# A two-layer hybrid block on one core: Strassen-like combinations of the hidden values in parts among the matmul steps, their low halves in the block after next

## The chip, the cores and the metric

One Trainium2 chip, one of its cores. The metric is the device time of one execution in microseconds (us). Three runs of the kernel before took 2234.09, 2236.21 and 2236.96 us; their median, 2236.21 us, is the time to compare with.

## The reference

256 tokens of width 2048 pass through two layers. Each layer has a mixer (gated delta rule and a linear recurrence in the first, two attentions in the second) and then a feed-forward part of inner width 5632. The change lies in the feed-forward part alone:

```python
def swiglu(hn, w_gate, w_up, w_down):
    return (jax.nn.silu(hn @ w_gate) * (hn @ w_up)) @ w_down
...
        h = h + swiglu(rmsnorm(h, ffn_norm[layer]), ffn_w_gate[layer], ffn_w_up[layer], ffn_w_down[layer])
```

## The kernel before, in words

All data are float32. Every product of float32 tiles is made of three matmuls on a high part (rounded by a ScalarE cast) and a low part (what the rounding left, a VectorE subtraction): high by high, high by low, low by high. `Bank.add` (L417 to L419) issues these three matmuls twice per weight tile and output bank.

The feed-forward part of a layer (`ffn`) is a stream of **blocks**. A block of gate and up weights makes 512 inner values for all tokens (`values`: silu(gate) times up). A block of down weights adds inner values times weights to 1024 of the 2048 output columns (`residual`). Per layer the stream has four gate and up blocks and two down blocks, again four and two, then three and one (16 blocks, numbered 0 to 15 here), and one more down block outside the stream.

Most blocks do part of their product with seven multiplications in place of eight (`seven`; called sevens below). That needs, besides sums of weight tiles (L483 and L490, VectorE, the tile "T"), four **combinations** of the left-hand values: `combine` makes them with four VectorE instructions of 128x256 (L396), a ScalarE cast for their high half (L397) and a VectorE subtraction for their low half (L399). For gate and up blocks the left-hand values are X and the combinations are made once a layer. For down blocks they are the inner values, and the combinations are made of the inner values of two, two and one of the blocks of a group: five a layer, ten in all.

`turned` does this for the values of a block j, in the next block. `first` transposes the values on TensorE (L654) and copies them out with ScalarE (L657 the high half of hid; L662 plain copies into the tile "e", only where combinations are wanted). `second` subtracts on VectorE for hid's low half (L666) and runs `combine` up to its `yield`, which stands behind the cast. `third` runs the rest, L399. These three are put ahead of steps 2, 3 and 4 of the block.

A block with two sevens has 22 **steps**, numbered 0 to 21 here: three plain ones, four steps of the sevens, a plain one, five of the sevens, a plain one, five of the sevens, three plain ones. A plain step is 12 matmuls, a step of a seven 6. `spread` puts functions ahead of the step of a given number, and `stream` issues all of it in the order that is written: inside `manual_schedule` VectorE, ScalarE and TensorE each take their instructions in this order. `stream` looks ahead: before step n is multiplied, the load, the sum T and the high cast (L530) of the steps up to n + 3 are issued, and the low subtraction (L543) of those up to n + 2. So a function put at n stands on VectorE behind the low part of step n + 1, and on ScalarE behind the cast of step n + 2.

Blocks 1, 2, 7, 8 and 13 of each layer hold combinations. Blocks 3, 9 and 14 of each layer have the same steps as gate and up blocks, but none.

The tile of the combinations and the sums T share a tag with two buffers (`mx.tile(..., tag="T", bufs=2)`). The values live in a tile "e" with one buffer, which the next block's values take at its step 20.

Of the kernel before, what the change touches and what calls it, by code (L numbers as in the profile page):

```python
# [47 lines left out]
def body(tc, A, out):  # L48
# [89 lines left out]
    def run(gen):  # L138

        while True:  # L140
            try:
                next(gen)
            except StopIteration as e:
                return e.value
# [244 lines left out]
    def combine(f, r=None):  # L389

        c = mx.tile([128, 4, 2, 128], F32, name="cc4", tag="T", bufs=2)
        if r is None:
            r = fp.tile([128, 2, 4, 2, 128], F32R, name="comb", tag="comb", bufs=4)
        a11, a21, a12, a22 = (f[t][:, 2 * j:2 * j + 2] for j in range(2) for t in range(2))
        for i, x, y, op in ((0, a21, a22, ALU.subtract), (1, a11, a21, ALU.subtract), (2, c[:, 0], a11, ALU.subtract), (3, a12, c[:, 2], ALU.add)):
            V.tensor_tensor(out=c[:, i], in0=x, in1=y, op=op)  # L396
        S.copy(r[:, 0], c)  # L397
        yield
        V.tensor_tensor(out=r[:, 1], in0=c, in1=r[:, 0].bitcast(F32), op=ALU.subtract)  # L399
        return r  # L400
# [237 lines left out]
    def ffn(L, then, fin=None):  # L638

        gu, dn = A[f"gu{L}"], A[f"dn{L}"]  # L640
        cx, ch, acts, guard = {}, {}, [], [None]
        todo = {}

        def turned(hid, j, want):

            o = {}

            def first():
                a = todo.pop(j)
                o["P"] = []  # L650
                for t in range(2):
                    P = ms([128, 4, 128], "Ph")
                    for i in range(4):
                        PE.transpose(P[:, i], a[:, 2 * t, i * 128:(i + 1) * 128], tb["ident"])  # L654
                    o["P"].append((P, hid[:, 4 * j:4 * j + 4, :, t * 128:(t + 1) * 128]))
                for P, d in o["P"]:
                    S.copy(d[:, :, 0], P)  # L657
                if want:

                    o["f"] = [a[:, 2 * t + 1].rearrange("p (k n) -> p k n", n=128) for t in range(2)]  # L660
                    for t in range(2):
                        S.copy(o["f"][t], o["P"][t][0])  # L662

            def second():
                for P, d in o["P"]:
                    V.tensor_tensor(out=d[:, :, 1], in0=P, in1=d[:, :, 0].bitcast(F32), op=ALU.subtract)  # L666
                if want:
                    o["c"] = combine(o["f"])
                    next(o["c"])

            def third():
                if want:
                    ch[j] = run(o["c"])

            return [first, second, third]

        def spread(order, put):

# [44 lines left out]

            return bank_sums, half(0), half(1)

        b, late, turn = 0, None, None
        for groups, down in (((0, 2, 2, 2), (2, 2)), ((2, 2, 2, 2), (2, 2)), ((2, 2, 2), (1, 1))):
            piece = len(groups)
            hid = ogp.tile([128, 16, 2, T], F32R, name="hid", tag="hid")
            for j in range(piece + 2):  # L730
                put = {}
                add = lambda n, *f: put.setdefault(n, []).extend(f)

                if late:
                    add(1, late)
                if turn:
                    for n, f in zip((2, 3, 4), turn):
                        add(n, f)
                late = turn = None
                if j < piece:  # L740
                    ns = groups[j]
                    order, F, M = steps(lambda i, u, b=b: gu[b, u, i], lambda k: X[:, k],
                                        {m: lambda m=m: cx[m] for m in range(ns)}, 4, 3, 3)
                    if b == 0:
                        add(5, lambda: cx.update({0: combine_x(X[:, 0:4])}))
                        add(8, rstd)
                        add(10, lambda: cx.update({1: combine_x(X[:, 4:8])}))
                    if b == 1:
                        guard[0] = order[0]
                    bs, h0, h1, late = values(hid, j, F, M, ns)  # L750
                    turn = turned(hid, j, j < max(down))
                    b += 1
                else:
                    p = j - piece
                    if b == NB and p == 1:
                        break
                    order, F, M = steps(lambda i, u, u0=2 * (b - piece), p=p: dn[2 * p + i, u0 + u], lambda k, hid=hid: hid[:, k],
                                        {m: lambda m=m: ch[m] for m in range(down[p])}, piece, 3, 3)
                    bs, h0, h1 = residual(p, F, M)
                n = len(order)  # L760
                add(n - 2, bs)
                add(n - 1, h0)
                spread(order, put)
                acts.append(h1)
# [3 lines left out]
        if fin:  # L768
            hooks, last = {5: lambda: then(0), 6: lambda: then(1)}, (3, 1, 3)
        else:  # L770
            hooks, last = {}, ()
# [763 lines left out]
```

## Time and profile before

| | |
|---|---|
| median of three runs | 2236.21 us |
| the profiled execution's own time | 2232.66 us |
| its span, first to last instruction | 2230.8 us |
| TensorE matmul busy | 2205.7 us (99%) |
| VectorE busy | 1965.3 us (88%) |
| ScalarE busy | 1333.4 us (60%) |
| mean granted TensorE clock | 0.999 of 2.4 GHz |

PE is TensorE, DVE VectorE, ACT ScalarE. A row of the timeline reads: start in us from the span's start, how long, engine, line, operation, output and inputs, shapes, how many instructions are merged; in brackets the idle time of the engine before it and what ended that. A matmul's end is modelled and overlaps the next one's start, so the pace of TensorE is read from start to start.

### The profile page before, as it was taken

What the parts mean: (1) busy time and instruction counts of PE and PEld (TensorE: products, weight loads), DVE (VectorE), ACT (ScalarE), POOL (GpSimd) and SP (SyncE); (2) the same over time, 40 slices, a digit from 0 to 9 for tenths busy, and PEclk for the clock granted to TensorE, in tenths of its full rate; (3) what the DMA queues carried; (4) which work ended last, traced back from release to release, by engine and by line L of the source; (5) the groups of instructions that cost most, each with busy time, mean ns of one, the idle gap of its engine ahead of it and who ended that gap; (6) DMA issues with size and microseconds to landing.
All of it is one profiled execution on the core that took longest, in us unless ns stands there. A gap on an engine that the chain in (4) does not pass through costs nothing.

```text
span 2230.8 us, 30548 instructions
## 1 busy us (share of the span) xinstructions
PE 2205.7 (99%) x10960; PEld 1838.8 (82%) x10960; DVE 1965.3 (88%) x2664; ACT 1333.4 (60%) x1784; POOL 54.0 (2%) x66
## 2 busy tenths in 40 slices
PE   9999999999999999999999999999999999999998
PEld 8888888877888778888888888888778887888786
DVE  8899676779999999999996688857899999999998
ACT  6776664556655666466664554445666566655665
POOL 0000000000000000000000000000000000000000
PEclk9999999999999999999999999999999999999999
DMA  8545456667778777778665565566678777877784
GB/s 284 156 144 168 141 147 187 208 190 229 226 229 247 205 219 235 224 219 238 198 199 155 157 185 174 161 181 226 189 212 232 229 215 225 237 222 232 223 238 151
DMA packets 126569, 453.78 MB, mean 203 GB/s; under 512 B 14129, under 2 KB 15665, under 8 KB 126289
## 3 DMA queue, kind: packets, MB, share of 16 engines
q1 hardware_dynamic: 117488, 420.10, 59.1%
q0 software_dynamic: 8640, 31.46, 8.7%
q8 instruction: 86, 1.41, 0.3%
q14 instruction: 67, 0.54, 0.1%
q10 hardware_dynamic: 288, 0.27, 0.0%
HBM read 449.68 MB, written 2.10 MB: 203 GB/s over the span
## 4 chain that ended last, share of the span: by engine, by line
PE 93%; DVE 4%; issue 1%; ACT 1%; DMA 0%; DVEq 0%; ACTq 0%
PE F L418 16%; PE F L419 16%; PE F L417 16%; PE Pw L201 11%; PE Pw L206 5%; PE M L418 5%; PE M L419 5%; PE M L417 4%; PE Px L305 3%; PE Px L307 3%; PE Px L306 3%; PE Ph L654 1%; DVE cc L396 1%; DVE tlo L543 1%; DVE T L490 1%
## 5 line engine op out<-in xcount | busy, mean ns | idle before, releaser
L181 ACT CAST whi<-raw 128x1024 fp32r<-128x1024 f32 x267 | 279.6, 1051 | 280.7 <-PE Pw L201 83.2
L182 DVE TENSOR_TENSOR wlo<-raw,whi 128x1024 fp32r<-128x1024 f32 x267 | 325.6, 1221 | 115.1 <-PE Px L306 37.9
L201 PE MATMUL Pw<-X,whi 128*128 128x512 f32 x1088 | 388.5, 400 | 0.0
L530 ACT CAST whi<-raw 128x1024 fp32r<-128x1024 f32 x342 | 350.7, 1047 | 33.5 <-PE F L419 16.9
L206 PE MATMUL Pw<-X,wlo 128*128 128x256 f32 x1088 | 304.7, 280 | 0.1
L417 PE MATMUL F<-whi,X 128*128 128x512 f32 x698 | 273.0, 391 | 0.0
L419 PE MATMUL F<-whi,X 128*128 128x512 f32 x698 | 272.2, 390 | 0.0
L543 DVE TENSOR_TENSOR wlo<-raw,whi 128x1024 fp32r<-128x1024 f32 x202 | 246.0, 1220 | 13.0 <-PE F L418 6.4
L418 PE MATMUL F<-wlo,X 128*128 128x512 f32 x650 | 254.1, 391 | 0.1
L530 ACT CAST whi<-T 128x1024 fp32r<-128x1024 f32 x110 | 116.0, 1055 | 213.4 <-DVE T L490 97.3
L201 PEld LDWEIGHTS Pw<-X,whi 128*128 128x128 f32 x1088 | 204.2, 188 | 47.4 <-issue 0.5
L206 PEld LDWEIGHTS Pw<-X,wlo 128*128 128x128 f32 x1088 | 205.3, 189 | 1.5 <-DVE wlo L182 0.8
L530 ACT CAST thi<-raw 128x1024 fp32r<-128x1024 f32 x162 | 169.4, 1047 | 12.0 <-PE F L419 8.8
L543 DVE TENSOR_TENSOR tlo<-raw,whi 128x1024 fp32r<-128x1024 f32 x140 | 170.8, 1220 | 5.6 <-PE F L418 3.0
L417 PEld LDWEIGHTS F<-whi,X 128*128 128x128 f32 x698 | 131.1, 188 | 27.0 <-issue 0.2
L419 PEld LDWEIGHTS F<-whi,X 128*128 128x128 f32 x698 | 131.1, 188 | 26.8
L530 ACT CAST thi<-T 128x1024 fp32r<-128x1024 f32 x64 | 67.5, 1054 | 132.4 <-DVE T L490 62.6
L418 PE MATMUL F<-tlo,X 128*128 128x512 f32 x370 | 144.5, 391 | 0.2 <-DVE tlo L379 0.2
L418 PEld LDWEIGHTS F<-wlo,X 128*128 128x128 f32 x650 | 122.1, 188 | 26.5 <-DVE wlo L543 1.8
L490 DVE TENSOR_TENSOR T<-T,raw 128x1024 f32<-128x1024 f32 x116 | 141.6, 1221 | 1.2
L417 PE MATMUL F<-whi,hid 128*128 128x512 f32 x352 | 137.8, 392 | 0.0
L419 PE MATMUL F<-whi,hid 128*128 128x512 f32 x352 | 137.1, 389 | 0.0
(448 smaller groups left out, 4688.6 us busy)
## 6 DMA issues: line engine op xcount, KB each, us to landing
raw<-in_gu SPq DMA_DIRECT2D x352, 512.0 KB, 4.5
raw<-in_dn SPq DMA_DIRECT2D x176, 512.0 KB, 4.8
raw<-in_w0w SPq DMA_DIRECT2D x72, 512.0 KB, 3.7
raw<-in_wo SPq DMA_DIRECT2D x64, 512.0 KB, 4.0
raw<-in_w1w SPq DMA_DIRECT2D x64, 512.0 KB, 3.7
raw<-in_gu POOLq DMA_DIRECT2D x40, 512.0 KB, 8.4
raw<-in_w1x SPq DMA_DIRECT2D x32, 512.0 KB, 4.2
raw<-in_dn POOLq DMA_DIRECT2D x20, 512.0 KB, 8.9
```

The lines of the kernel that those rows point to most:

```text
L181: S.copy(hi, raw)
L182: V.tensor_sub(lo, raw, hi.bitcast(F32))
L201: PE.matmul(P.rearrange("p a b -> p (a b)"), hi[:, kk], X[:, k].rearrange("p a b -> p (a b)"), start=k == 0, stop=False)
L206: PE.matmul(P[:, 0], lo[:, kk], X[:, k, 0], start=False, stop=k == NK - 1)
L305: PE.matmul(Ps[t], x[:, 0, ts], hi[:, kk], start=k == 0, stop=False)
L306: PE.matmul(Ps[t], x[:, 0, ts], lo[:, kk], start=False, stop=False)
L417: PE.matmul(self.t, xh, hi[:, kk], start=self.i == kk == 0, stop=False)
L418: PE.matmul(self.t, xh, lo[:, kk], start=False, stop=False)
L419: PE.matmul(self.t, xl, hi[:, kk], start=False, stop=kk == 1 and self.i == self.n - 1)
L490: V.tensor_tensor(out=b["t"], in0=b["t"], in1=b[name], op=ALU.add)
L530: S.copy(y.hi, y.raw)
L543: V.tensor_sub(y.lo, y.raw, y.hi.bitcast(F32))
```

## The change

`combine` yields also behind its second and its third VectorE instruction. `turned` now returns two things: functions with their step numbers for the next block (first at 2, second at 3, and, where combinations are wanted, a part at 8 and a part at 14), and a function for step 2 of the block after that one. So `second` makes two of the four combinations, the third follows ahead of step 8, the fourth and the cast ahead of step 14, and the low half one block later, behind that block's own `first`.

```diff
--- before.py
+++ after.py
@@ -394,6 +394,8 @@
         a11, a21, a12, a22 = (f[t][:, 2 * j:2 * j + 2] for j in range(2) for t in range(2))
         for i, x, y, op in ((0, a21, a22, ALU.subtract), (1, a11, a21, ALU.subtract), (2, c[:, 0], a11, ALU.subtract), (3, a12, c[:, 2], ALU.add)):
             V.tensor_tensor(out=c[:, i], in0=x, in1=y, op=op)
+            if 0 < i < 3:
+                yield
         S.copy(r[:, 0], c)
         yield
         V.tensor_tensor(out=r[:, 1], in0=c, in1=r[:, 0].bitcast(F32), op=ALU.subtract)
@@ -668,11 +670,14 @@
                     o["c"] = combine(o["f"])
                     next(o["c"])
 
-            def third():
-                if want:
-                    ch[j] = run(o["c"])
-
-            return [first, second, third]
+            def part():
+                next(o["c"])
+
+            def last():
+                ch[j] = run(o["c"])
+
+
+            return {2: first, 3: second, **({8: part, 14: part} if want else {})}, [last] if want else []
 
         def spread(order, put):
 
@@ -723,7 +728,7 @@
 
             return bank_sums, half(0), half(1)
 
-        b, late, turn = 0, None, None
+        b, late, turn, rest, next_rest = 0, None, None, [], []
         for groups, down in (((0, 2, 2, 2), (2, 2)), ((2, 2, 2, 2), (2, 2)), ((2, 2, 2), (1, 1))):
             piece = len(groups)
             hid = ogp.tile([128, 16, 2, T], F32R, name="hid", tag="hid")
@@ -733,10 +738,11 @@
 
                 if late:
                     add(1, late)
-                if turn:
-                    for n, f in zip((2, 3, 4), turn):
-                        add(n, f)
-                late = turn = None
+                for n, f in (turn or {}).items():
+                    add(n, f)
+                add(2, *rest)
+                late, turn, rest = None, None, next_rest
+                next_rest = []
                 if j < piece:
                     ns = groups[j]
                     order, F, M = steps(lambda i, u, b=b: gu[b, u, i], lambda k: X[:, k],
@@ -748,7 +754,7 @@
                     if b == 1:
                         guard[0] = order[0]
                     bs, h0, h1, late = values(hid, j, F, M, ns)
-                    turn = turned(hid, j, j < max(down))
+                    turn, next_rest = turned(hid, j, j < max(down))
                     b += 1
                 else:
                     p = j - piece
```

The arithmetic and the instructions are the same; TensorE's, SyncE's and GpSimd's orders are unchanged. What moves on VectorE is shown for blocks 2 and 3 of the first layer. In the changed file the numbers of the lines that follow are higher: L543 becomes L545, L490 L492, L483 L485, L399 L401, L666 L668, L702 L707.

The first place is VectorE around steps 3 to 6 of block 2, first before:

```order
L543 TENSOR_TENSOR tlo<-raw_5329,whi 128x1024
L543 TENSOR_TENSOR wlo<-T,whi 128x1024
L666 TENSOR_TENSOR hid<-Ph,hid 128x4x128 x2
L396 TENSOR_TENSOR cc_5407<-e 128x256 x2
L396 TENSOR_TENSOR cc_5407<-cc_5407,e 128x256
L396 TENSOR_TENSOR cc_5407<-e,cc_5407 128x256
L490 TENSOR_TENSOR T<-T,raw_5387 128x1024
L543 TENSOR_TENSOR tlo<-raw_5387,thi 128x1024
L399 TENSOR_TENSOR comb<-cc_5407,comb 128x1024
L543 TENSOR_TENSOR wlo<-T,whi 128x1024
```
and now:

```order
L545 TENSOR_TENSOR tlo<-raw_5328,whi 128x1024
L401 TENSOR_TENSOR comb<-cc_5051,comb 128x1024
L545 TENSOR_TENSOR wlo<-T,whi 128x1024
L668 TENSOR_TENSOR hid<-Ph,hid 128x4x128 x2
L396 TENSOR_TENSOR cc_5407<-e 128x256 x2
L492 TENSOR_TENSOR T<-T,raw_5387 128x1024
L545 TENSOR_TENSOR tlo<-raw_5387,thi 128x1024
L545 TENSOR_TENSOR wlo<-T,whi 128x1024
```
The last two of the four combinations and their low half have left this place; the low half of the previous block's combinations (cc_5051) has come in ahead of step 4's low part.

The second place is VectorE around steps 9 to 16 of block 2, first before:

```order
L543 TENSOR_TENSOR wlo<-T,whi 128x1024
L543 TENSOR_TENSOR tlo<-raw,whi 128x1024
L483 TENSOR_TENSOR T<-raw_5480,raw 128x1024
L543 TENSOR_TENSOR wlo<-raw_5480,thi 128x1024
L543 TENSOR_TENSOR wlo<-T,whi 128x1024
L543 TENSOR_TENSOR tlo<-raw_5507,whi 128x1024
L490 TENSOR_TENSOR T<-T,raw 128x1024
L543 TENSOR_TENSOR wlo<-raw,thi 128x1024
L543 TENSOR_TENSOR tlo<-T,whi 128x1024
L490 TENSOR_TENSOR T<-T,raw_5543 128x1024
L543 TENSOR_TENSOR wlo<-raw_5543,whi 128x1024
```
and now:

```order
L545 TENSOR_TENSOR wlo<-T,whi 128x1024
L396 TENSOR_TENSOR cc_5407<-cc_5407,e 128x256
L545 TENSOR_TENSOR tlo<-raw,whi 128x1024
L485 TENSOR_TENSOR T<-raw_5477,raw 128x1024
L545 TENSOR_TENSOR wlo<-raw_5477,thi 128x1024
L545 TENSOR_TENSOR wlo<-T,whi 128x1024
L545 TENSOR_TENSOR tlo<-raw_5504,whi 128x1024
L492 TENSOR_TENSOR T<-T,raw 128x1024
L545 TENSOR_TENSOR wlo<-raw,thi 128x1024
L545 TENSOR_TENSOR tlo<-T,whi 128x1024
L396 TENSOR_TENSOR cc_5407<-e,cc_5407 128x256
L492 TENSOR_TENSOR T<-T,raw_5540 128x1024
```
The third combination stands behind step 9's low part, the fourth behind step 15's and ahead of the sum and of the low part of step 16 (`wlo<-raw_5540`, the row after the last one shown).

The third place is the start of block 3, which has no combinations, first before:

```order
L543 TENSOR_TENSOR tlo<-raw_5685,whi 128x1024
L543 TENSOR_TENSOR wlo<-T,thi 128x1024
L666 TENSOR_TENSOR hid<-Ph,hid 128x4x128 x2
L490 TENSOR_TENSOR T<-T,raw 128x1024
L543 TENSOR_TENSOR wlo<-raw,whi 128x1024
```
and now:

```order
L545 TENSOR_TENSOR tlo<-raw_5684,whi 128x1024
L401 TENSOR_TENSOR comb<-cc_5407,comb 128x1024
L545 TENSOR_TENSOR wlo<-T,thi 128x1024
L668 TENSOR_TENSOR hid<-Ph,hid 128x4x128 x2
L492 TENSOR_TENSOR T<-T,raw 128x1024
L545 TENSOR_TENSOR wlo<-raw,whi 128x1024
```
Here the low half of block 2's combinations (cc_5407) is one more instruction ahead of step 4's low part and of hid's low halves.

## Rows read from the trace of the kernel before

**Rows 1.** The page, part 1: TensorE's busy time, share and instructions.

```profile
PE 2205.7 (99%) x10960; PEld 1838.8 (82%) x10960; DVE 1965.3 (88%) x2664; ACT 1333.4 (60%) x1784; POOL 54.0 (2%) x66
```

**Rows 2.** Waits of TensorE: who waited for whom, us in total, times, longest.

```profile
PE M L418 <- DVE wlo L543: 3.7, 6, 0.6
PE F L418 <- DVE tlo L543: 3.6, 6, 0.6
...
PE M L418 <- DVE tlo L543: 2.4, 4, 0.6
PE F L418 <- DVE wlo L543: 2.4, 4, 0.6
```

**Rows 3.** Timeline of TensorE, block 2 of the first layer, steps 5 and 6.

```profile
531.01 0.39 PE L419 MATMUL M<-whi,comb 128*128 128x512 f32 x1
531.24 0.39 PE L417 MATMUL F<-thi,comb 128*128 128x512 f32 x1
532.22 0.50 PE L418 MATMUL F<-tlo,comb 128*128 128x512 f32 x1 [0.59 <-DVE tlo L543]
532.55 0.40 PE L419 MATMUL F<-thi,comb 128*128 128x512 f32 x1
...
533.48 0.39 PE L417 MATMUL M<-whi,comb 128*128 128x512 f32 x1
534.49 0.50 PE L418 MATMUL M<-wlo,comb 128*128 128x512 f32 x1 [0.62 <-DVE wlo L543]
```

**Rows 4.** Timeline of TensorE, the same block, step 16.

```profile
550.98 0.48 PE L418 MATMUL F<-wlo,X 128*128 128x512 f32 x1
551.30 0.40 PE L419 MATMUL F<-whi,X 128*128 128x512 f32 x1
```

**Rows 5.** Timeline of VectorE, the same block, steps 3 to 6, then 9 to 12.

```profile
523.68 1.22 DVE L543 TENSOR_TENSOR tlo<-raw,whi 128x1024 fp32r<-128x1024 f32 x1
524.97 1.23 DVE L543 TENSOR_TENSOR wlo<-T,whi 128x1024 fp32r<-128x1024 f32 x1
527.14 1.29 DVE L666 TENSOR_TENSOR hid<-Ph,hid 128x512 fp32r<-128x512 f32 x2 [0.95 <-ACT e L662]
...
529.01 0.42 DVE L396 TENSOR_TENSOR cc<-cc,e 128x256 f32<-128x256 f32 x1
529.47 0.42 DVE L396 TENSOR_TENSOR cc<-e,cc 128x256 f32<-128x256 f32 x1
529.81 1.22 DVE L490 TENSOR_TENSOR T<-T,raw 128x1024 f32<-128x1024 f32 x1
530.95 1.22 DVE L543 TENSOR_TENSOR tlo<-raw,thi 128x1024 fp32r<-128x1024 f32 x1
532.08 1.22 DVE L399 TENSOR_TENSOR comb<-cc,comb 128x1024 fp32r<-128x1024 f32 x1
533.22 1.22 DVE L543 TENSOR_TENSOR wlo<-T,whi 128x1024 fp32r<-128x1024 f32 x1
...
537.90 1.23 DVE L543 TENSOR_TENSOR wlo<-T,whi 128x1024 fp32r<-128x1024 f32 x1
...
540.17 1.22 DVE L483 TENSOR_TENSOR T<-raw,raw 128x1024 f32<-128x1024 f32 x1
```

**Rows 6.** Timeline of ScalarE, the same block: the combinations' cast and the next.

```profile
529.93 1.05 ACT L397 CAST comb<-cc 128x1024 fp32r<-128x1024 f32 x1 [1.39 <-DVE cc L396]
531.06 1.05 ACT L530 CAST whi<-T 128x1024 fp32r<-128x1024 f32 x1
```

**Rows 7.** Timeline of VectorE, block 3: the low parts of steps 5 and 16.

```profile
572.18 1.22 DVE L543 TENSOR_TENSOR wlo<-raw,whi 128x1024 fp32r<-128x1024 f32 x1
...
589.93 1.22 DVE L543 TENSOR_TENSOR tlo<-raw,thi 128x1024 fp32r<-128x1024 f32 x1
```

**Rows 8.** Timeline of TensorE, block 3: the matmuls that take these two low parts.

```profile
575.12 0.39 PE L418 MATMUL F<-wlo,comb 128*128 128x512 f32 x1
...
592.80 0.39 PE L418 MATMUL F<-tlo,X 128*128 128x512 f32 x1
```

## The prediction

> **What bounds the kernel now.** I read the page's busy times first: TensorE is busy for 2205.7 us of the 2230.8 us span, 99% [rows 1]. So at most 25.1 us lie in gaps that the page can see, and a change that leaves TensorE's instructions alone can only give back stalls. The second view is what TensorE waits for. In the feed-forward parts that is almost only VectorE's low parts of weight tiles (L543), 6 + 6 + 4 + 4 = 20 times, 3.7 + 3.6 + 2.4 + 2.4 = 12.1 us [rows 2]. Twenty is two for each of the ten blocks that make combinations, so the third view is the timeline of one of them, block 2 of the first layer. TensorE's pace there is 0.23 us from matmul to matmul (531.01 to 531.24). At step 5 it takes 0.98 us to the next start, 0.75 too many, and the one after that comes 0.33 later, 0.10 too many; at step 6 the gap is 1.01 us, 0.78 too many, and I count the same 0.10 behind it [rows 3]. At step 16 another gap is 0.32 us, 0.09 too many [rows 4]. Together 0.75 + 0.10 + 0.78 + 0.10 + 0.09 = **1.82 us per block, 18.2 us in ten**. That is more than the view of waits gives, since the modelled end of a matmul hides part of a stall; from here on I count starts.
>
> Why these steps: the low part of step 5 ends at 530.95 + 1.22 = 532.17 and TensorE starts at 532.22, 0.05 later [rows 3, 5]. Ahead of it VectorE has done hid's low halves, four combinations and a sum without a pause. The low part of step 6 stands behind the combinations' low half, L399. In block 3, which has the same steps but no combinations, the low part of step 5 ends at 573.40 and is taken at 575.12, 1.72 us later; at step 16 these are 591.15 and 592.80, 1.65 us [rows 7, 8]. So over these eleven steps VectorE's work and TensorE's are almost equal: the distance shrinks by 0.07 us. A block that is late at step 5 stays late; VectorE has no room in the middle of a block, and this decides what the change is worth.
>
> **The change, part by part.** The sum is made against the profiled execution, 2232.66 us; the median of the three runs is 3.55 us above it, and I take the saving from the median.
>
> *Out of steps 3 to 6.* Two of four combinations leave the place ahead of the sum. From the start of the third to that of the sum pass 529.81 - 529.01 = 0.80 us [rows 5]. The start of this stretch does not move, since L666 waits for ScalarE's copies there, which follow TensorE's transposes. So the low part of step 5 ends at 532.17 - 0.80 = 531.37, where TensorE without a stall wants it at 531.24 + 0.23 = 531.47: 0.10 us of room, 0.05 of which the handing over needs. The first stall goes, narrowly. L399 costs 533.22 - 532.08 = 1.14 us [rows 5], so step 6 is earlier by 0.80 + 1.14 = 1.94 us, against the 1.63 us (0.75 + 0.10 + 0.78) by which TensorE was held up there: the second stall goes too. ScalarE does not keep it: before, the cast of the sum began at 531.06, just after the sum's end at 531.03 and behind the combinations' cast [rows 5, 6]; now that cast is gone from there and the sum ends earlier.
>
> *Into steps 9 to 16.* Two combinations of 128x256 come in, one ahead of step 10's low part, one ahead of step 16's. Start to start such a one costs 529.81 - 529.47 = 0.34 us where the next does not wait for its result, and 529.47 - 529.01 = 0.46 where it does [rows 5]. What follows now is a weight tile's low part or sum, which does not, so I take 0.34, and keep 0.46 as the upper end; below, 0 would be one that hides in a pause, and rows 5 show VectorE without pauses between these steps, so I price that as a rival. By block 3's shape the room at step 16 is 0.10 - 0.07 - 2 x 0.34 = -0.65 us. With 0.05 to hand over and 0.10 for the restart, TensorE is held up by **0.80 us per block** in place of 1.82, at step 16, or in part some steps earlier, which does not change the total. That saves **1.02 us per block, 10.2 us in ten**.
>
> *The cast* of the combinations (L397, 1.05 us) now stands on ScalarE between the casts of steps 16 and 17. The cast of step 17 needs a sum that VectorE makes behind the fourth combination; that sum ends 0.34 + 1.22 - 0.42 = 1.14 us after the combination, and the cast of 1.05 us, begun 0.04 after it (529.93 against 529.47 + 0.42), is over by then, as it was in its old place [rows 5, 6]. I cost it at nothing; uncovered it would be 1.05 us.
>
> *The low half, one block on.* L399 stands ahead of step 4's low part and hid's low halves of the next block. In blocks 2 and 8 VectorE is idle for 0.95 us right behind step 4's low part, until ScalarE has copied [rows 5]. Step 3's low part starts at 523.68; with 1.14 for L399 step 4's starts at about 525.95 and is over at 527.18, and L666 starts at 527.14 now: covered to within a few hundredths. In blocks 3, 9 and 14 nothing covers it and everything behind is later by up to 1.14 us, but there TensorE's room is 1.65 us and more [rows 7, 8]. So nothing, in ten places. If the four blocks 2 and 8 of both layers had to pay it in full, it would be 4 x (1.14 + 0.10) = 5.0 us: the upper end.
>
> *What else is touched.* The combinations' tile now keeps one of the two T buffers into the next block, so the sevens' sums share the other. In block 2 the second seven's first sum starts at 540.17, and the last reader of the previous T is over at 537.90 + 1.23 = 539.13 [rows 5]: no wait. The values in "e" are read until ahead of step 14, and the tile is taken again at step 20. The queues of SyncE and GpSimd keep their order; a weight tile's buffer comes free up to 0.34 us later behind the pieces.
>
> **The sum.** 2232.66 - 10.2 = 2222.5 us for an execution like the profiled one, 2236.21 - 10.2 = **2226.0 us** for the median.
>
> **The rivals.** *A, every stall goes:* the pieces fall into pauses. Then 18.2 us come back, 2218.0 us. For it: the large stalls are at steps 5 and 6 alone. Against it: the 0.09 us at step 16 [rows 4] and the distance that shrinks from 1.72 to 1.65 in block 3 show that the middle has no pauses.
>
> *B, a piece costs its whole duration.* Two runs of VectorE's instructions overlap at their seams now: the combinations last 0.42 us and start 0.34 apart, L399 lasts 1.22 and the next starts after 1.14 [rows 5]. Should a piece between unlike instructions lose that overlap, each costs 0.42 or more, the stall grows by 2 x 0.08 = 0.16 us per block, and 1.6 us of the saving are lost: 2227.6 us; at 0.46 it is 0.24, and 2228.4. The Trainium skill has such a rule: in VectorE: DVE Perf Modes, section The DRAIN you can't avoid, the next instruction does not start until the pipe has emptied, so that only the number of instructions counts. The starts in this trace do not agree with it as it stands, being closer than the durations.
>
> *C, the low half is not covered one block on.* Its place is ahead of step 4's low part, its price 1.14 + 0.10 us, and it decides where the next block has less room than that. Paid in all ten next blocks it is 12.4 us, more than the 10.2 saved: 2236.2 + 2.2 = 2238.4 us, slower. For it: it stands ahead of hid's low halves, and steps 5 and 6 come right behind. Against it: 0.95 us of idle time in blocks 2 and 8, 1.65 us of room in the others [rows 5, 7, 8]. The four full prices alone give 2231.0 us.
>
> *D, nothing is won:* the stalls move whole to later steps. It would need the low half, too, to stay in its block; it leaves it, as the order shows. What stays of this case is that something unseen, such as a later landing of a weight tile, eats the saving: about 2236 us.
>
> **How the numbers follow.** Forecast 0.74, A 0.06, B 0.10, C 0.04, D 0.06. The range runs from 2222.0 (4 us under the forecast, as the three runs lie within 2.9 us of each other and the profiled one 3.55 under their median) to 2231.0, which takes in B and the four uncovered blocks; it leaves out A, C and D, 0.16. A measurement of this kernel can tell about 0.2%, 4.5 us, from no change. Faster by more than that, below 2231.7 us: the forecast, A and B, 0.90. Within it: most of D and half of C, 0.07. Slower: the rest, 0.03.
>
> **What would show it.** Right: in the ten blocks TensorE's gaps at steps 5 and 6 are gone or under 0.2 us, and gaps of 0.6 to 0.8 us in all stand at steps 11 to 16; VectorE's busy time unchanged; blocks 3, 9 and 14 as long as before. A shows as no gap at step 16. B shows as VectorE starting 0.42 or more after each lone combination. C shows as new gaps at steps 5 or 6 of blocks 2, 3, 8, 9 and 14. The forecast is wrong if the low part of step 5 is still waited for by more than 0.3 us, or if the gap at step 16 passes 1.5 us.

## The result and the profile after

Six runs of the changed kernel took 2220.22 to 2223.29 us, median **2220.81 us**; six of the kernel before on the same chip 2232.10 to 2236.96, median 2235.15. The ratio is 0.9939, 95% interval 0.9926 to 0.9952: faster by 14.3 us by the medians (10.7 to 16.5 by the interval), where 10.2 were forecast. The direction and the mechanism hold, two sizes in the sum do not; the time lies 5.2 us under the forecast and 1.2 us under the range.

The page's busy times first: TensorE is busy as long as before, in a span 9.3 us shorter [rows 1].

```profile
PE 2205.5 (99%) x10960; PEld 1840.4 (83%) x10960; DVE 1961.7 (88%) x2664; ACT 1332.7 (60%) x1784; POOL 54.0 (2%) x66
```

What TensorE waits for (the same columns as [rows 2]), in the feed-forward parts:

```profile
PE F L420 <- DVE wlo L545: 0.8, 1, 0.8
PE F L419 <- DVE h L725: 0.7, 1, 0.7
```

The twenty waits for low parts, 12.1 us, are gone; one of 0.8 us is left, and one of 0.7 for a sum (h, L725), to which I come at the end of this section. So where a block still loses time must be read from starts. The timeline of TensorE in block 2 of the changed kernel, the block's first matmul, then steps 5, 11 and 16, and the first matmuls of blocks 3 and 4:

```profile
518.97 0.39 PE L419 MATMUL F<-whi,X 128*128 128x512 f32 x1
...
530.74 0.39 PE L419 MATMUL F<-thi,comb 128*128 128x512 f32 x1
530.97 0.46 PE L420 MATMUL F<-tlo,comb 128*128 128x512 f32 x1
531.27 0.40 PE L421 MATMUL F<-thi,comb 128*128 128x512 f32 x1
...
540.58 0.50 PE L420 MATMUL M<-wlo,X 128*128 128x512 f32 x1
540.92 0.40 PE L421 MATMUL M<-thi,X 128*128 128x512 f32 x1
...
548.69 0.39 PE L419 MATMUL F<-whi,X 128*128 128x512 f32 x1
549.16 0.50 PE L420 MATMUL F<-wlo,X 128*128 128x512 f32 x1
549.50 0.40 PE L421 MATMUL F<-whi,X 128*128 128x512 f32 x1
...
561.40 0.39 PE L419 MATMUL F<-whi,X 128*128 128x512 f32 x1
...
603.10 0.39 PE L419 MATMUL F<-thi,hid 128*128 128x512 f32 x1
```

And the first matmuls of blocks 2, 3 and 4 in the kernel before:

```profile
519.46 0.39 PE L417 MATMUL F<-whi,X 128*128 128x512 f32 x1
...
563.12 0.39 PE L417 MATMUL F<-whi,X 128*128 128x512 f32 x1
...
604.82 0.39 PE L417 MATMUL F<-thi,hid 128*128 128x512 f32 x1
```

Block 3, without combinations, takes 41.70 us in both (563.12 to 604.82; 561.40 to 603.10). Block 2 took 43.66, 1.96 more, and takes 42.43, 0.73 more. Call this the **excess** of a block with combinations over one without. It is what the combinations cost TensorE, whether in gaps that one sees or in hundredths that one does not. I worked it out for all ten blocks, from the first to the last matmul start of each (41.47 us without combinations): before the ten sum to 20.1 us, typically 2.00; in the changed kernel to 7.1, typically 0.67. The difference, **13.0 us**, is what these blocks give back.

The gaps of block 2: 0.07 too many at step 5 (531.27 after 530.97), 0.11 at step 11, 0.24 and 0.11 at step 16; the rest of its excess is hundredths. The 0.75 and 0.78 of before [rows 3] are gone here. In block 2 of the second layer 0.25 and 0.11 us are left at step 5, and its excess is 0.98. VectorE in block 2 of the first layer, steps 3 to 6, then the two moved combinations:

```profile
524.36 1.22 DVE L401 TENSOR_TENSOR comb<-cc,comb 128x1024 fp32r<-128x1024 f32 x1
525.49 1.22 DVE L545 TENSOR_TENSOR wlo<-T,whi 128x1024 fp32r<-128x1024 f32 x1
526.65 1.29 DVE L668 TENSOR_TENSOR hid<-Ph,hid 128x512 fp32r<-128x512 f32 x2
527.85 0.75 DVE L396 TENSOR_TENSOR cc<-e 128x256 f32<-128x256 f32 x2
528.52 1.22 DVE L492 TENSOR_TENSOR T<-T,raw 128x1024 f32<-128x1024 f32 x1
529.66 1.22 DVE L545 TENSOR_TENSOR tlo<-raw,thi 128x1024 fp32r<-128x1024 f32 x1
...
536.70 0.42 DVE L396 TENSOR_TENSOR cc<-cc,e 128x256 f32<-128x256 f32 x1
537.04 1.22 DVE L545 TENSOR_TENSOR tlo<-raw,whi 128x1024 fp32r<-128x1024 f32 x1
...
545.28 1.23 DVE L545 TENSOR_TENSOR tlo<-T,whi 128x1024 fp32r<-128x1024 f32 x1
546.42 0.42 DVE L396 TENSOR_TENSOR cc<-e,cc 128x256 f32<-128x256 f32 x1
546.75 1.22 DVE L492 TENSOR_TENSOR T<-T,raw 128x1024 f32<-128x1024 f32 x1
```

The low half L401 of the previous block ends at 525.58, step 4's low part at 526.71, and hid's low halves start at 526.65, with no idle time ahead of them: the 0.95 us of [rows 5] is used up almost to the hundredth, as the prediction had it. The low part of step 5 ends at 530.88 and is taken at 530.97: 0.09 us of room, where 0.10 was forecast.

In block 3 VectorE and TensorE stand like this at step 5:

```profile
571.58 1.22 DVE L545 TENSOR_TENSOR wlo<-raw,whi 128x1024 fp32r<-128x1024 f32 x1
```
```profile
573.40 0.39 PE L420 MATMUL F<-wlo,comb 128*128 128x512 f32 x1
```

The low part ends at 572.80 and is taken at 573.40: the room of 1.72 us [rows 7, 8] has become 0.60, less by 1.12, the price of the low half (1.14), and nothing waits.

The one wait of 0.8 us that is left in the view of waits is of block 15 of the second layer, and no work of the change: there ScalarE, ahead of the copies of the transposed values, waits for a transfer of the last norm's weights:

```profile
2154.81 1.92 ACT L1385 ACTIVATE fin<-fin 128x2048 f32<-128x2048 f32 x1 [2.85 <-DMA fin<-in_fw]
```

That made this execution's block 15 33.55 us long in place of 31.95, and it is the slowest of the six (2223.29). Over all the executions profiled here ScalarE waits for this transfer between nothing and 2.85 us; it is a part of what runs of one kernel differ by. The 0.7 us for L725 stand in the block outside the stream at the second layer's end. From its first matmul to its last it takes 32.08 us here and 31.97 when the kernel is run again, 31.20 before: 0.8 to 0.9 us of the saving are lost there. No run took this apart.

### The profile page after: what moved, and what is told of

It is laid out like the page before. It is cut to its first block, busy times and chain, and to the rows that moved or that the text cites. A ratio compares the mean times of both kernels' runs of the same rounds, so it can differ in the third digit from the quotient of the medians.

```text
span 2221.5 us, 30558 instructions
## 1 busy us (share of the span) xinstructions
PE 2205.5 (99%) x10960; PEld 1840.4 (83%) x10960; DVE 1961.7 (88%) x2664; ACT 1332.7 (60%) x1784; POOL 54.0 (2%) x66
## 3 DMA queue, kind: packets, MB, share of 16 engines
q8 instruction: 86, 1.41, 0.3%
## 4 chain that ended last, share of the span: by engine, by line
PE 85%; DVE 7%; issue 4%; ACT 2%; DMA 1%; DVEq 0%; ACTq 0%; SPq 0%
PE F L420 14%; PE F L421 14%; PE F L419 14%; PE Pw L201 11%; PE Pw L206 6%; PE M L421 4%; PE M L420 4%; PE M L419 4%; PE Px L305 3%; PE Px L307 3%; PE Px L306 3%; DVE T L492 2%; DVE wlo L545 1%; ACT thi L532 1%; DVE tlo L545 1%
## 5 line engine op out<-in xcount | busy, mean ns | idle before, releaser
L545 DVE TENSOR_TENSOR wlo<-raw,whi 128x1024 fp32r<-128x1024 f32 x202 | 245.9, 1219 | 13.7 <-PE F L420 6.8
L545 DVE TENSOR_TENSOR tlo<-raw,whi 128x1024 fp32r<-128x1024 f32 x140 | 170.6, 1219 | 6.0 <-PE F L420 3.3
L492 DVE TENSOR_TENSOR T<-T,raw 128x1024 f32<-128x1024 f32 x116 | 141.5, 1220 | 0.9
```

The source lines that it names most:

```text
L492: V.tensor_tensor(out=b["t"], in0=b["t"], in1=b[name], op=ALU.add)
L545: V.tensor_sub(y.lo, y.raw, y.hi.bitcast(F32))
```

## The experiments

After the result the first theory is the prediction's own account with its sizes mended: VectorE's room, counted in hundredths, decides; what stands ahead of step 5 or 16 beyond it is paid by TensorE. The other ways are a gain that comes from one part of the change alone, and moved work that is free wherever it stands. The diffs are against the changed kernel. A gap is given as two numbers: at the low part, and behind it at the restart. Ratios are to the runs of the kernel before on the same chip. Their intervals are 4 to 6 us wide, so several of the kernels below cannot be told apart by their times; what tells them apart is the excess of their blocks.

### The changed kernel once more

> The changed kernel once more. Theory 1 (all of the gain lies in the ten blocks with combinations, whose length over a block without fell from 1.97 us to 0.70 us, and nothing else moved): 13 us less than before, ratio 0.994; the ten blocks again about 42.15 us from first to last matmul, and block 15 of the second layer 32.0 us as before, not the 33.6 us of the first profile. Theory 2 (the profiled span, 9.3 us shorter, is the right measure, and the changed kernel loses some 3 us elsewhere): ratio 0.996, and block 15 long again.

Measured: 2221.05 us, ratio 0.9945 (0.9932 to 0.9957), 13.0 us less than the 2234.03 of before there. The excess of the ten blocks sums again to 7.1 us, and block 15 has its 31.95. So the time and the blocks give the same saving here, as far as the interval (9.6 to 15.2 us) can say.

### Each part of the change alone

All four combinations back at step 3, only the low half one block on:

```diff
-            if 0 < i < 3:
-                yield
...
-            return {2: first, 3: second, **({8: part, 14: part} if want else {})}, [last] if want else []
+            return {2: first, 3: second, **({} if want else {})}, [last] if want else []
```

> Only the low half moved to the block after next; all four combinations and the cast stay ahead of step 4. Theory 1 (VectorE's work ahead of each step decides): the stall at step 5 stays, 0.75 + 0.1 us; that at step 6 goes; about 0.1 at step 16; about 1.05 us per block in place of 1.97, so 9 us less than before, 4 us more than the change. Rival (both parts are needed, the debt of step 5 comes back at step 6): under 4 us less than before.

Measured: 2224.37 us, 0.9959 (0.9945 to 0.9973). Step 5 has its old gap of 0.76 and 0.11 us, the one at step 6 is gone, the excess is typically 0.94. That is 3.3 us more than the change on the same chip, where the theory had 4.

Only the two combinations moved, the low half in the same block behind them:

```diff
-            return {2: first, 3: second, **({8: part, 14: part} if want else {})}, [last] if want else []
+            return {2: first, 3: second, **({8: part, 14: part, 15: last} if want else {})}, []
```

> The combinations in parts as in the change, but the low half ahead of step 15 of the same block. Theory 1: steps 5 and 6 without stalls; the 1.14 us of the low half come due at step 17, a stall of some 0.9 us besides the one at step 16; 1.6 to 1.7 us per block, so 3 us less than before. Rival (it is the spreading that counts, wherever the low half stands): as the change, 13 us less.

Measured: 2228.60 us, 0.9977 (0.9968 to 0.9986), excess 1.56. The gap at step 16 is that of the change (0.25 and 0.11), and the low half makes one more at step 17, 0.76 to 0.78 and 0.11. Against the change the low half in its own block costs 0.9 us a block. Over the ten blocks the excess sums to 20.1 us before, 15.5 with the combinations moved alone, 9.7 with the low half alone, 7.1 with both. So the low half is worth 8 to 10 us of the 13, the combinations 3 to 5, and neither alone has it all.

### What the low half's cover is worth

The low half issued twice in the next block, so that a second instruction of the same size finds the cover used:

```diff
-        V.tensor_tensor(out=r[:, 1], in0=c, in1=r[:, 0].bitcast(F32), op=ALU.subtract)
+        for _ in range(1 if first else 2):
+            V.tensor_tensor(out=r[:, 1], in0=c, in1=r[:, 0].bitcast(F32), op=ALU.subtract)
...
-                    o["c"] = combine(o["f"])
+                    o["c"] = combine(o["f"], first=False)
```

> The change with the low half's instruction issued twice, both in the block after next. Theory (one of them is covered in blocks 2 and 8 by VectorE's idle time ahead of hid's low halves and leaves 0.5 to 0.6 us of room in blocks 3, 9 and 14): the second is paid in full in blocks 2 and 8, 1.14 us at step 5, and by 0.6 us in blocks 3, 9 and 14; 4 x 1.14 + 6 x 0.6 = 8 us more than the change. Rival (VectorE has more room at the start of a block than the trace of before shows): under 3 us more.

Measured: 2229.38 us, 0.9983 (0.9974 to 0.9992). By the ratios that is 8 to 10 us more than the change, and by the blocks' lengths 9.3. TensorE in block 2 of this kernel:

```profile
529.25 0.39 PE L420 MATMUL F<-thi,comb 128*128 128x512 f32 x1
530.66 0.50 PE L421 MATMUL F<-tlo,comb 128*128 128x512 f32 x1 [1.02 <-DVE tlo L546]
531.00 0.40 PE L422 MATMUL F<-thi,comb 128*128 128x512 f32 x1
```

From 529.25 to 530.66 are 1.41 us, 1.18 too many (1.39, 1.21 and 1.29 in the other three blocks 2 and 8), and 0.11 follow: the second low half (1.14) is paid in full. In blocks 3, 9 and 14 the gap is 0.5 and 0.11: the 0.60 us of room that the change left there cannot hold 1.14. This is rival C's mechanism at its price. The change itself escapes it because of the 0.95 us of idle time and the 1.65 us of room, which the prediction named.

### Where the combinations stand

Third and fourth as late as they go, at steps 18 and 19:

```diff
-            return {2: first, 3: second, **({8: part, 14: part} if want else {})}, [last] if want else []
+            return {2: first, 3: second, **({18: part, 19: part} if want else {})}, [last] if want else []
```

> The change with its third and fourth combinations ahead of steps 18 and 19 in place of 8 and 14. Theory 1 (the 0.5 us of gaps that are left at steps 11 and 16 are the two combinations that stand ahead of them, and the plain steps 19 to 21 have 2 us of room and more): gaps at steps 11 and 16 under 0.15 us, 0.1 to 0.2 us per block in place of 0.70, so 5 us less than the change and 18 less than before, ratio 0.992. Rival (the end of the block is as full: the values' tile, its sums and the casts wait there): gaps at steps 20, 21 or ahead of the transposes, and no better than the change.

Measured: 2235.19 us, 1.0006 (0.9997 to 1.0015), the whole gain lost. The combinations cost their own block next to nothing now (excess 0.12 to 0.17 in blocks 1, 7 and 13), but the block behind each has a gap at step 5: 1.67 and 0.11 us in blocks 2 and 8, 1.0 and 0.11 in 3, 9 and 14. It also starts late, by 0.24 us or more. Three timelines of this kernel show why: ScalarE and VectorE at the end of block 1, TensorE at the start and at step 5 of block 2.

```profile
510.53 1.05 ACT L399 CAST comb<-cc 128x1024 fp32r<-128x1024 f32 x1 [1.58 <-DVE cc L396]
...
512.43 0.58 ACT L431 COPY e<-M 128x512 f32<-128x512 f32 x1
```
```profile
513.04 0.69 DVE L432 TENSOR_TENSOR e<-M,e 128x512 f32<-128x512 f32 x1 [1.41 <-ACT e L431]
```
```profile
517.67 0.47 PE L419 MATMUL F<-whi,X 128*128 128x512 f32 x1
...
529.56 0.39 PE L419 MATMUL F<-thi,comb 128*128 128x512 f32 x1
531.46 0.50 PE L420 MATMUL F<-tlo,comb 128*128 128x512 f32 x1 [1.50 <-DVE tlo L545]
```

ScalarE waits 1.58 us for the fourth combination, casts it, and comes late to the copy e (L431) that VectorE needs for the sums of the block's output; VectorE stands idle 1.41 us. Some 0.4 us of lateness show at once: block 2's first matmul starts at 517.67, 0.53 us after the one before it (517.14), and the next one 0.08 late. The rest waits until step 5, 18 us on. So VectorE has hardly any spare time across the boundary either.

To tell the idle time from the work itself, the same with the cast behind that copy, each part one yield further. What stands at step 21 is the cast. The expectation says the low half, but that stays one block on, as in the change:

```diff
-            if 0 < i < 3:
+            if i > 0:
                 yield
...
-            return {2: first, 3: second, **({8: part, 14: part} if want else {})}, [last] if want else []
+            return {2: first, 3: second, **({18: part, 19: part, 21: part} if want else {})}, [last] if want else []
```

> Third combination at step 18, fourth at 19, the low half at step 21, each part behind one yield more, so that on ScalarE the cast of the combinations stands behind the copy of the next block's combination e. Theory (in the run with third and fourth at 18 and 19 it was the cast, waiting for the fourth combination ahead of that copy, that left VectorE idle 1.41 us at the block's end, and that idle time came due at step 5): the idle time is gone, the gaps at step 5 of the next blocks fall from 1.67 and 1.0 us to 0.4 or less and to none, the blocks with combinations stay near 41.6 us, and the time is about 3 to 4 us below the change's, near 2217 to 2218. Rival (late VectorE work is itself the debt, wherever the cast stands): the gap at step 5 stays at 1.0 us or more and the time is no better than before the change.

Measured: 2221.62 us, 0.9937 (0.9923 to 0.9951), no better than the change. The idle time of 1.41 us is gone, and so is the late start of the blocks behind. The gap at step 5 falls to 0.57 to 0.91 us and the restart in blocks 2 and 8, and to 0.24 or less in 3, 9 and 14, but not to nothing. TensorE at step 5 of block 2:

```profile
529.03 0.39 PE L419 MATMUL F<-thi,comb 128*128 128x512 f32 x1
530.02 0.50 PE L420 MATMUL F<-tlo,comb 128*128 128x512 f32 x1 [0.60 <-DVE tlo L545]
```

In this block, of the 1.67 us the idle time was 0.9, and 0.77 (530.02 less 529.03 and 0.23 is 0.76) are about two combinations at 0.34 each. With the 0.4 at the block's start the idle time comes to 1.3 of its 1.41 us. Both theories are half right: an order on ScalarE made VectorE idle, and late work is itself a debt to the next block.

### What one combination costs

In the changed kernel the third combination starts 0.34 us before the next instruction, the fourth 0.33 (rows above). But the fourth pushes the sum behind it by less. In the kernel before, the same place on VectorE reads:

```profile
546.01 1.22 DVE L543 TENSOR_TENSOR wlo<-raw,thi 128x1024 fp32r<-128x1024 f32 x1
547.29 1.23 DVE L543 TENSOR_TENSOR tlo<-T,whi 128x1024 fp32r<-128x1024 f32 x1
548.55 1.23 DVE L490 TENSOR_TENSOR T<-T,raw 128x1024 f32<-128x1024 f32 x1
```

These start 1.28 and 1.26 us apart, where instructions of this size otherwise start 1.13 to 1.14 apart [rows 5]. The view calls no idle time there, yet 0.14 us pass ahead of the low part of a sum T, and 0.12 ahead of a sum that takes in and writes a T while the instruction before still reads one. What the first waits for can be read from ScalarE, here in the changed kernel, where this low part starts at 545.28:

```profile
544.19 1.05 ACT L532 CAST whi<-T 128x1024 fp32r<-128x1024 f32 x1 [1.74 <-DVE T L492]
```

The sum's cast ends at 545.24, 0.04 us ahead of it. What the second waits for I infer from the names; no run took it apart. In the changed kernel low part, combination and sum take 546.75 - 545.28 = 1.47 us: 0.21 more than 1.26, not 0.34. Such a **pause** takes in 0.13 of a combination's 0.34. Three kernels test this.

The third at step 7 in place of 8, ahead of a low part of a T:

```diff
-            return {2: first, 3: second, **({8: part, 14: part} if want else {})}, [last] if want else []
+            return {2: first, 3: second, **({7: part, 14: part} if want else {})}, [last] if want else []
```

> The change with the third combination ahead of step 7 in place of 8, so that on VectorE it stands ahead of step 9's low part and not behind it. Theory 1 (a lone combination costs the 0.34 us between starts wherever it stands in the full middle of the block): as the change, 0.67 us per block over a block without combinations. Theory 2 (the middle has small pauses: 0.14 us ahead of a low part that waits for the cast of its sum, 0.12 us ahead of a sum that waits for the low part before it; a combination that stands in one costs 0.20 us): 0.53 us per block, 1.4 us less than the change in all; in the timeline the low part of step 9 starts 1.47 to 1.49 us after that of step 8, in place of 1.28 plus 0.34.

Measured: 2219.53 us, 0.9936 (0.9923 to 0.9950). The gap at step 11 is gone, and in block 2 the low part of step 9 starts 1.47 us after that of step 8, as theory 2 has it. The excess is typically 0.54; three blocks keep 0.19 to 0.30 us at step 5, so the ten sum to 6.1 us, 0.9 less than the change.

Both in places without a pause (the same line with 5 and 11):

> The change with the two later combinations ahead of steps 5 and 11, places without a pause on VectorE. Theory 1: as the change, 0.67 us per block. Theory 2 (in the change one of the two stands in a pause): each costs 0.34 us here, 0.80 us per block, some 1.3 us more than the change in all, with the gaps earlier in the block.

Measured: 2222.48 us, 0.9950 (0.9938 to 0.9963); 0.37 and 0.11 at step 16, the excess typically 0.81, in ten blocks 8.9 us.

All four apart, one in each pause, none ahead of step 5:

```diff
-            if 0 < i < 3:
+            if i < 3:
                 yield
...
                     o["c"] = combine(o["f"])
-                    next(o["c"])
...
-            return {2: first, 3: second, **({8: part, 14: part} if want else {})}, [last] if want else []
+            return {2: first, 3: second, **({7: part, 10: part, 13: part, 14: part} if want else {})}, [last] if want else []
```

> All four combinations apart, ahead of steps 7, 10, 13 and 14: three ahead of a low part that waits for a cast, one ahead of a sum that waits for a low part; none ahead of step 5. Theory 2: four times 0.20 us in place of 0.67 + 0.34 + 0.20, so 0.2 to 0.4 us per block in place of 0.67, with a gap at step 16 alone, 3 to 4 us less than the change. Theory 1: four times 0.34 us, no better than the change, since two of them only move from ahead of step 5 to ahead of step 16.

Measured: 2218.03 us, 0.9930 (0.9917 to 0.9942), the excess typically 0.22: 0.05 and 0.11 at step 16 and some hundredths. Two blocks of the second layer lie above it (block 2 with 0.53, block 8 with 0.35). The ten sum to 2.6 us, the least of the versions tried. It was run again beside the last one below:

> The kernel with combinations at steps 7, 10, 13 and 14 once more, beside the one with one of them ahead of step 3, on the same chip. Theory: 0.993 of the time before, as in its first run, blocks with combinations 41.67 to 41.71 us. Rival (its first run was a favourable one): 0.995 or more.

Measured: 2217.47 us, 0.9928 (0.9914 to 0.9941), excess 0.23, in ten blocks 2.5 us. By the ratios of its two runs it takes about 16 us less than the kernel before and 2 to 4 less than the change; the intervals of the two overlap, the blocks' 2.5 and 7.1 us do not. VectorE around steps 13 to 16 of block 2 in this second run, then TensorE at step 16:

```profile
541.94 1.22 DVE L545 TENSOR_TENSOR wlo<-raw,thi 128x1024 fp32r<-128x1024 f32 x1
543.08 0.42 DVE L396 TENSOR_TENSOR cc<-cc,e 128x256 f32<-128x256 f32 x1
543.41 1.22 DVE L545 TENSOR_TENSOR tlo<-T,whi 128x1024 fp32r<-128x1024 f32 x1
544.55 0.42 DVE L396 TENSOR_TENSOR cc<-e,cc 128x256 f32<-128x256 f32 x1
544.88 1.22 DVE L492 TENSOR_TENSOR T<-T,raw 128x1024 f32<-128x1024 f32 x1
```
```profile
547.00 0.39 PE L419 MATMUL F<-whi,X 128*128 128x512 f32 x1
547.29 0.50 PE L420 MATMUL F<-wlo,X 128*128 128x512 f32 x1
547.62 0.40 PE L421 MATMUL F<-whi,X 128*128 128x512 f32 x1
```

From 541.94 to 543.41 are 1.47 us and from 543.41 to 544.88 again 1.47: 0.19 and 0.21 over the pauses' own 1.28 and 1.26. Two combinations for 0.40 us.

### Two tries to better it

The fourth at step 15, behind step 16's low part (the parts at 7, 10, 13 and 15):

> Combinations at steps 7, 10, 13 and 15, all in places where a low part waits for the cast of its sum anyway, low half as in the change. Theory (a combination costs only what its instruction exceeds the pause it fills): against the kernel with 7, 10, 13 and 14 the last gap, 0.05 and 0.11 us at step 16, goes, the excess of a block with combinations falls from 0.20-0.24 to 0.05-0.15 us, and the time falls by about 1 to 1.5 us, near 2216.7. Rival (the late combination has no slack left behind it): the gap moves to step 17 or 18 and the time is no better than with 7, 10, 13 and 14.

Measured: 2223.62 us, 0.9948 (0.9936 to 0.9961), worse, with an excess of 0.88 to 0.90 in blocks 1, 7 and 13 and of 1.15 to 1.17 in 2 and 8. Step 16's gap is gone from the first, in the others 0.12 and 0.11 us stay, and all ten blocks have a new one at step 18, 0.66 and 0.11 us. VectorE, ScalarE and TensorE there:

```profile
547.50 1.22 DVE L545 TENSOR_TENSOR wlo<-T,thi 128x1024 fp32r<-128x1024 f32 x1
549.65 1.23 DVE L545 TENSOR_TENSOR tlo<-raw,whi 128x1024 fp32r<-128x1024 f32 x1 [0.93 <-ACT whi L532]
```
```profile
547.62 1.05 ACT L399 CAST comb<-cc 128x1024 fp32r<-128x1024 f32 x1 [0.34 <-DVE cc L396]
548.57 1.99 ACT L532 CAST whi<-raw 128x1024 fp32r<-128x1024 f32 x2
```
```profile
550.04 0.40 PE L419 MATMUL M<-whi,comb 128*128 128x512 f32 x1
550.93 0.50 PE L420 MATMUL M<-tlo,comb 128*128 128x512 f32 x1 [0.49 <-DVE tlo L545]
```

Here the combinations' cast stands in front of the cast of step 18's weight tile, which needs no VectorE work; with the fourth at 14 it was not waited for. That cast is the first of the two merged in the row that follows, and VectorE idles 0.93 us for it. My theory looked at VectorE alone. The rival named the right step, but its reason, no slack behind the late combination, is not what the rows show: it is ScalarE's order.

One combination at step 3, the others at 7, 10 and 13 (a `yield` behind the first three, parts at these steps):

> One combination ahead of step 3, the others ahead of steps 7, 10 and 13, so that each of these three stands in a place where the next low part waits for the cast of its sum, and the cast of the combinations stands ahead of that of step 16, where the fourth at 13 leaves room. Low half as in the change. Theory (a combination is paid by what it exceeds the pause it fills; behind the last of them the cast must find ScalarE with room): the gap at step 16 that the four at 7, 10, 13 and 14 leave (0.05 and 0.11 us) goes, step 5 keeps about 0.34 us more room than in the change, the excess of a block with combinations falls from 0.20-0.24 to 0.10 us or less, and the time lies 1 to 2 us below that of the kernel with 7, 10, 13 and 14. Rival (the cast, one step earlier, is waited for at step 16 or 17 as it was at 18 with the fourth at 15): a gap of 0.5 us or more there, and a time no better than the change's.

Measured: 2218.81 us, 0.9932 (0.9920 to 0.9945), excess typically 0.36, with 0.18 and 0.11 us at step 16: more than all four apart, not less. ScalarE isn't waited for; the combination ahead of step 5 stands in no pause and costs its whole 0.34, which I had left out.

### One sum for all of them

With the parts measured, a block's excess follows from an addition, made afterwards and no forecast. At step 5 the change has 0.09 us of room with two combinations ahead, so 0.77 with none; up to step 16 0.07 is lost [rows 7, 8], which leaves 0.70. A combination costs 0.34 without a pause, 0.46 where it waits for the one before [rows 5], 0.20 in a pause. What goes beyond the room, with 0.05 to hand over and 0.10 to restart, is the excess:

| combinations at | their sum | less 0.70, plus 0.15 | measured, typical block |
|---|---|---|---|
| 3 (all four) | 0.68 + 0.46 + 0.34 = 1.48 | 0.93 | 0.94 |
| 3, 3, 5, 11 | 4 x 0.34 = 1.36 | 0.81 | 0.81 |
| 3, 3, 8, 14 (the change) | 3 x 0.34 + 0.20 = 1.22 | 0.67 | 0.67, 0.68 |
| 3, 3, 7, 14 | 2 x 0.34 + 2 x 0.20 = 1.08 | 0.53 | 0.54 |
| 3, 7, 10, 13 | 0.34 + 3 x 0.20 = 0.94 | 0.39 | 0.36 |
| 7, 10, 13, 14 | 4 x 0.20 = 0.80 | 0.25 | 0.22, 0.23 |

The sum is for the typical block. In five of the six kernels block 2 of the second layer lies 0.3 us above it, and one or two others lie above it here and there; what holds these up is not traced. The low half is one block on in all six. The three kernels with combinations at 15, 18 or 19 are outside the sum: there ScalarE's order or the next block pays.

## Why the prediction was right, and where it was wrong

*What bounds the kernel:* right. What is saved is stalls of TensorE in ten blocks; blocks 3, 9 and 14 have their old length to the hundredth. What the prediction did not have is the 0.8 to 0.9 us that the block at the second layer's end takes longer.

*Out of steps 3 to 6:* right. Both stalls are gone in nine of ten blocks, with 0.09 us of room at step 5 of block 2 against 0.10. That the first one went "narrowly" shows in block 2 of the second layer, where 0.25 and 0.11 us are left.

*The stall before, 1.82 us per block:* too small, the first of the two steps that failed and the larger. I added the gaps that are seen as such at steps 5, 6 and 16. The block's length against one without combinations gives 1.96 in block 2 and 20.1 us in ten, in place of 18.2. Missing in my sum are hundredths of a microsecond at many matmuls that TensorE takes just behind VectorE, 0.10 to 0.17 us a block, and block 1 of the first layer, whose gap at step 16 is 0.24 and 0.11 us, not 0.09.

*Into steps 9 to 16, 0.80 us per block:* too large. The second step that failed is the price of the fourth combination, 0.34, and the sentence it rests on, that rows 5 show VectorE without pauses between these steps. They hold none that the view calls idle; starts 1.26 and 1.28 apart in place of 1.14 were a pause, and I had read only the stretch at steps 10 to 12. The third combination, in no pause, cost the full 0.34; the fourth 0.21. Measured: 7.1 us in ten blocks in place of 8.0. The gaps that one sees at steps 11 to 16 come to 0.44 to 0.52 us, under the 0.6 to 0.8 that were named as the sign.

Together 1.9 + 0.9 = 2.8 us, which makes 10.2 into 13.0. Of the 5.2 us by which the time missed, 1.1 more are the base: I started from the median of three runs, 2236.21, and six gave 2235.15. The last 1.3 lie inside the interval of the ratio and are not traced, nor are the 0.8 to 0.9 that the last block loses. That the range began only 4 us under the forecast was wrong for the same reason: it held the scatter of the runs but no error of the 1.82, which I took for read when it was counted from a part of its rows.

*The cast, at nothing:* right in this place. The last experiments show how little it lacked: one step later it costs 0.66 and 0.11 us a block, at steps 18 and 19 for the third and fourth it makes VectorE idle 1.41 us.

*The low half, at nothing:* right in all ten places, by the cover that was named.

*The rivals.* A, every stall goes: not at these steps; but all four apart come within 2.5 us of it in ten blocks, by what A says, pieces that fall into pauses. B is wrong: lone pieces between unlike instructions start 0.34 and 0.33 us before the next. The Trainium skill's page VectorE: DVE Perf Modes has, beside the section named in the prediction, one called Two Vector instructions with no wait between them, by which a held instruction starts only when every earlier one has finished; the section named in the prediction says itself that one that is not held starts earlier. These starts agree with that, and not with that section's first rule read by the durations in the profile; no run here varied what holds an instruction. C happens only where the cover is taken away, at its price. D's hidden transfer did not show in the ten blocks; a small one, of the last norm's weights, cost the first profile's block 15 its 1.6 us.

## What to carry to other kernels

Price a bound stretch by its length against the same stretch without the suspect work, not by adding the gaps one can see. Before work is moved, look for pauses by starts: where neighbours of one size start later than usual, a small instruction costs only what it exceeds the pause, here 0.20 us in place of 0.34. And follow the moved work's consumers on the other in-order engine: a cast that was free behind one step cost 0.77 us behind the next.

## What the runs showed of the hardware

A VectorE instruction of 128x1024 that needs ScalarE's cast of a sum just made starts 1.28 us behind the one before it in place of 1.14, and a sum behind an instruction that still reads a T 1.26, without idle time in the view. When a matmul of TensorE has waited for a low part, be it 0.06 us (547.29) or 1.18 (530.66), the next starts 0.33 to 0.34 us after it in place of 0.23, so that a wait of 0.06 us cost 0.1 us more. And of an idle time of VectorE, 1.41 us, TensorE paid some 0.4 us at the next block's start and 0.9 only 18 us later, at the next place where its room was small.
